# Weight copies tied to a place behind the probabilities' copies, and one transposed key half moved to another bank

## The chip, the cores and the metric

The program runs on one core of a Trainium2 chip. The metric is the device time of one execution in microseconds (us). Three runs of the kernel before gave 1273.09, 1273.96 and 1275.84 us; their median, 1273.96 us, is the time before. PE is the matrix engine, DVE the vector engine, ACT the scalar engine, POOL the general one, SP the queue from which all DMAs here are issued. The work of each engine is done in the order of its own queue; engines wait for each other by semaphores.

## The reference

Two layers work on 256 latent tokens and, in the first layer, 256 context tokens, of width 1024. Each layer is a half-step SwiGLU block, a mixer, and a second half-step SwiGLU block; a modulation from a conditioning vector goes in ahead of each, a residual and a LayerNorm stand behind it. The mixer of the first layer is attention, that of the second a short gated convolution. The change lies in the attention:

```python
qkv = (hx @ w_qkv)                      # 16 heads of 64
q, k = apply_axial_rope(q), apply_axial_rope(k)
qkv_c = (hc @ w_qkv)                    # the context's keys and values
s_win = q k^T * scale + bias, masked    # the neighbourhood: 256 keys with a mask
s_ctx = q k_c^T * scale                 # 256 context keys
p = softmax(concat([s_win, s_ctx]))
o = p[..., :nk] v_blk + p[..., nk:] v_c
y_lat = o.reshape(B, S, D) @ w_out      # the output projection
```

The result is the latent stream, 256 by 1024.

## The kernel before

**Precision.** Every large product is made of two halves: an operand x is split into hi, a copy rounded by the scalar engine, and lo = x - hi, a subtraction on the vector engine. A product is then three matmuls, hi·hi (L159), hi·lo (L160) and lo·hi (L162), added up in one bank of the sums (PSUM). `mmu` issues them: for a pair of row blocks hi·hi and hi·lo twice in turn, then lo·hi twice.

**Weights.** `wunit` (L165) brings one unit of weights: a DMA of 512 KB into a raw tile (tag wr, 4 buffers), two copies of 128x512 on ACT (L181) and two subtractions of 128x512 on DVE (L184). A raw buffer is free for the next DMA when the second subtraction has read it. The DMAs stand in one queue on SP, so one that waits for a raw buffer holds those behind it, the bias tiles' (L738) among them.

**Attention.** The loop at L914 goes over 32 steps, a step being one head and one half of the queries. Scores of two heads (`scores`) go to two banks of the tag "at" (3 banks); the vector engine adds the bias (L830) and takes the maximum (L832), the scalar engine makes the exponentials (L834), the vector engine a reciprocal (L835), and the scalar engine scales the row (L836). Two steps later `probs_T` transposes the probabilities of that step on PE into a bank of the tag "tp" (2 banks) as four 128x128 transposes (L848), and splits them: an ACT copy (L108) and a DVE subtraction (L109). One step on, `values` multiplies them with the values (L860, L861) into a bank of "mm" (3 banks) and adds up two halves (L866, L867).

**What fills PE between.** Between these steps `fill_some` takes matmuls from a generator: first the products for keys and values (`kv_quarter`, names wkv) and queries (`q_half`, wq), then, from step 24 on, the output projection (`last_filler`, wo). A unit of weights is requested where its first matmul is written. `kv_quarter` ends with `rest`, which transposes the keys in two halves j = 0, 1 (kT) into "tp" banks and splits them.

**Order.** The order on PE is the order in which the code is written (manual_schedule). On the other engines a scheduler sets the order: it goes by priorities, and `high_priority` moves weight copies (W_EARLY = 40) and probabilities (P_EARLY = 70) ahead of others. Weight copies so come early or late by what the scheduler believes to be free.

Of the kernel before, what the change touches and what calls it, by code (L numbers as in the profile page):

```python
# [16 lines left out]
P = 128  # L17
# [49 lines left out]
def backbone_kernel(  # L67
# [19 lines left out]
    w_early = [0]  # L87
    ext = [1, 0]
    ada_late = [0]

    def nm(s):
        uid[0] += 1
        return f"{s}_{uid[0]}"

    def act(dt=F32, s="a"):
        return ap.tile([P, 512], dt, tag="act", name=nm(s))

    def bank(tag, s):
        return pp.tile([P, 512], F32, tag=tag, bufs=PB[tag], name=nm(s))

    def mmb(s="mm", t=0):
        return bank("at" if t % 2 else "mm", s)

    def tpb(s="tp"):
        return bank("tp", s)

    def split(src, hi, lo):
        a = nc.scalar.activation(hi, src, AF.Copy)  # L108
        return a, nc.vector.tensor_tensor(out=lo, in0=src, in1=hi.bitcast(F32), op=ALU.subtract)  # L109
# [55 lines left out]
    def wunit(srcs, kn, s):  # L165

        raw = wp.tile([P, UN], F32, tag="wr", bufs=WB[0], name=nm(s + "r"))
        ext[1] += 1
        if ext[0] and ext[1] % (5 + ext[0]) in (E0 if ext[0] == 1 else E2):
            hi = hp.tile([P, UN], F32R, tag="whx", bufs=ext[0], name=nm(s + "h"))  # L170
            lo = hp.tile([P, UN], F32R, tag="wlx", bufs=ext[0], name=nm(s + "l"))
        else:
            hi = wp.tile([P, UN], F32R, tag="wh", bufs=WB[1], name=nm(s + "h"))
            lo = wp.tile([P, UN], F32R, tag="wl", bufs=WB[2], name=nm(s + "l"))
        rv, hv, lv = (t[:, :kn * 512].rearrange("p (a b) -> p a b", a=kn) for t in (raw, hi, lo))
        with tc.high_priority(offset=w_early[0]):
            for src, c in srcs:
                sync.dma_start(rv[:, :, c:c + src.shape[2]], src)
            m = kn * 512
            for a in range(0, m, m // W_HI):  # L180
                nc.scalar.activation(hi[:, a:a + m // W_HI], raw[:, a:a + m // W_HI], AF.Copy)  # L181
            for a in range(0, m, m // W_LO):
                b = a + m // W_LO
                nc.vector.tensor_tensor(out=lo[:, a:b], in0=raw[:, a:b], in1=hi[:, a:b].bitcast(F32), op=ALU.subtract)  # L184
        return hv, lv

    def wrows(w, r0, n, c0, s):
        src = w[r0:r0 + n * P, c0:c0 + 512].rearrange("(k p) n -> p k n", p=P)
        return wunit([(src, 0)], n, s)
# [25 lines left out]
    pt = tpb("ctp")  # L215
# [357 lines left out]
    for q, (k0, n) in enumerate(steps):  # L573
        nxt = start_step(*steps[q + 1]) if q < 4 else iter(())
        for g in range(6):
# [6 lines left out]
            p, j, z = g // 4, g // 2 % 2, g % 2  # L582
# [66 lines left out]
    def sub_end(w, lhs, nk, l, i, gm, wgt, nxt, s, order):  # L649


        gate = mod_rows(l, gm, "gate")
        lnr = None if nxt else ln_rows(l, i)
        GB = fold_cols(nxt[0], 0, nxt[1], (l, i)) if nxt else None
        st, hTs = {}, [None, None]

        def evac(t, n, bank, *c):
            if n == 0:
                st[t] = stat_tile(2 if nxt or t == 0 else 3)
            part = nxt is None and t == n == 1  # L660
            cs = slice(*(c or (0, 512)))
            residual(bank, xt[t][n][:, cs], gate[n][:, cs], wgt, None if c else ALPHA,
                     None if part and not c else st[t][:, n + (c[0] // 256 if c else 0)])
            if n == 1 and (not part or c and c[1] == 512):
                mv, rs = finish_stats(st[t])
                if nxt:
                    hTs[t] = modulated(xt[t], mv, rs, GB, (LN_LAG if nk > KC else LT_LAG)[t], t == 0)
                else:
                    for h in range(2):
                        nc.vector.scalar_tensor_tensor(out=xt[t][h], in0=xt[t][h], scalar=mv[:, 0:1], in1=lnr[0][h],  # L670
                                                       op0=ALU.subtract, op1=ALU.mult)
                    for h in range(2):
                        nc.vector.scalar_tensor_tensor(out=xt[t][h], in0=xt[t][h], scalar=rs, in1=lnr[1][h],
                                                       op0=ALU.mult, op1=ALU.add)
                        sync.dma_start(out[0, t * P:(t + 1) * P, h * 512:(h + 1) * 512], xt[t][h])

        return out_gemm(w, lhs, nk, order, evac, s), hTs, (lambda: new_x(l, i))
# [31 lines left out]
    def rtile(n):  # L709
        if n == 256:  # L710
            return hp.tile([P, n], F32, tag="kr", bufs=8, name=nm("kr"))
        return sp.tile([P, n], F32, tag="s2", bufs=S2, name=nm("qr"))

    def roped(src, t, which, nh):
        n = nh * HD
        C = rope[:, t, 2 * which, :]
        S = rope[:, t, 2 * which + 1, :].rearrange("p (a b e) -> p a b e", a=2, b=2)
        r1 = rtile(n)
        r2 = sp.tile([P, n], F32, tag="tmp", bufs=3, name=nm("r2"))
        nc.vector.tensor_tensor(out=r1.rearrange("p (h d) -> p h d", h=nh), in0=src.rearrange("p (h d) -> p h d", h=nh),  # L720
                                in1=C.unsqueeze(1).to_broadcast([P, nh, HD]), op=ALU.mult)
        bv = src.rearrange("p (h a b e) -> p h a b e", h=nh, a=2, b=2)
        rv = r2.rearrange("p (h a b e) -> p h a b e", h=nh, a=2, b=2)
        for b in range(2):
            nc.vector.tensor_tensor(out=rv[:, :, :, b, :], in0=bv[:, :, :, 1 - b, :],
                                    in1=S[:, :, b, :].unsqueeze(1).to_broadcast([P, nh, 2, 16]), op=ALU.mult)
        nc.vector.tensor_tensor(out=r1, in0=r1, in1=r2, op=ALU.add)
        return r1
# [19 lines left out]
    def tile_panel(c0, c1, hl, s, each):  # L748

        units = []  # L750
        for t, hT in enumerate(hl):
            bk = mmb(s)
            for u in range(KU):
                if t == 0:
                    units.append(wpair(w_qkv, u, c0, c1, s))
                hi, lo = units[u]
                mmu(bk, [(*hsl(hT, UK * u + i), hi[:, i], lo[:, i]) for i in range(UK)], u == 0, u == KU - 1)
                if u == KU - 1:
                    with tc.high_priority(offset=ROPE_EARLY):
                        each(t, bk)  # L760
                yield
                tick()

    def kv_quarter(g, res):
        krs, v = [], []

        def each(t, bk):
            if t < 2:
                krs.append(roped(bk[:, 0:256], t, 1, 4))
            else:  # L770
                r1 = rtile(256)
                nc.scalar.activation(r1, bk[:, 0:256], AF.Copy)
                krs.append(r1)
            v.append(act(F32R, "v"))
            z = v[t].rearrange("p (h s d) -> p h s d", h=4, s=2)
            split(bk[:, 256:512].rearrange("p (h d) -> p h d", h=4), z[:, :, 0], z[:, :, 1])

        yield from tile_panel(D + g * 256, 2 * D + g * 256, [hTs[t] for t in range(4)], "wkv", each)

        def rest():  # L780
            kT = []
            for j in range(2):
                ps = tpb("kT")
                for t in range(4):
                    nc.tensor.transpose(ps[:, t * P:(t + 1) * P], krs[t][:, j * P:(j + 1) * P], ident)
                hi, lo = act(F32R, "kTh"), act(F32R, "kTl")
                split(ps, hi, lo)
                kT.append((hi, lo))
            return kT

        res.append((Late(1, rest), v))
# [50 lines left out]
    def probs_T(h, qt, pr):  # L842
        if h not in PT:
            PT[h] = [hp.tile([P, 4, 256], F32R, tag="pt", bufs=4, name=nm("pT")) for _ in range(2)]
        pth, ptl = PT[h]
        pt = tpb("PT")
        for k in range(4):
            nc.tensor.transpose(pt[:, k * P:(k + 1) * P], pr[:, k * P:(k + 1) * P], ident)  # L848
        split(pt.rearrange("p (k q) -> p k q", k=4), pth[:, :, qt * P:(qt + 1) * P], ptl[:, :, qt * P:(qt + 1) * P])

    osum = {}

# [61 lines left out]
    for i in range(len(steps) + LAG + V_LAG):  # L914
# [24 lines left out]
        j = i - LAG - V_LAG  # L939
# [4 lines left out]
    run(fin)  # L944
    phase.__exit__(None, None, None)
    hTs, later = box
    phase = tc.tile_pool(name="ph2", bufs=1)
    hp = phase.__enter__()
    bias_rows.clear()
# [65 lines left out]
    g, hTs, later = sub_end(sc_w_out[0], lhs_T(yT), KC, 1, 1, 5, 1.0, (1, 6), "wo", order_late(KU))  # L1015
# [57 lines left out]
```

## Time and profile before

| what | us |
|---|---|
| median of three runs | 1273.96 |
| the profiled execution, its own time | 1274.29 |
| span of its trace, first to last instruction | 1272.5 |
| PE idle from 447 to 520 of the span | 0.39 |
| PE idle from 520 to 600 of the span | 8.28 |
| PE idle from 600 to 1272 of the span | 11.20 |

The attention with its fill lies between about 380 and 600 us. The profiled execution stands 0.33 us above the median, and 1.79 us of it lie outside the span. The idle rows are the length of a stretch less PE's busy time in it. A row of a time order gives the start, the duration, the engine, the line, the operation, output<-inputs, and, in brackets, how long the engine was idle just before and what ended that. Matmuls overlap: one of 128x512 shows some 0.39 us, and the next begins some 0.23 us after its start.

### The profile page before, as it was taken

What the parts mean: (1) busy time and instruction counts of PE and PEld (TensorE: products, weight loads), DVE (VectorE), ACT (ScalarE), POOL (GpSimd) and SP (SyncE); (2) the same over time, 40 slices, a digit from 0 to 9 for tenths busy, and PEclk for the clock granted to TensorE, in tenths of its full rate; (3) what the DMA queues carried; (4) which work ended last, traced back from release to release, by engine and by line L of the source; (5) the groups of instructions that cost most, each with busy time, mean ns of one, the idle gap of its engine ahead of it and who ended that gap; (6) DMA issues with size and microseconds to landing.
All of it is one profiled execution on the core that took longest, in us unless ns stands there. A gap on an engine that the chain in (4) does not pass through costs nothing.

```text
span 1272.5 us, 17210 instructions
## 1 busy us (share of the span) xinstructions
PE 1243.8 (98%) x5890; PEld 1005.1 (79%) x5890; DVE 954.3 (75%) x1681; ACT 590.5 (46%) x1148; POOL 42.8 (3%) x71
## 2 busy tenths in 40 slices
PE   7999999999999999988999999999999999999997
PEld 4787778787878777766787788778788887888786
DVE  3699887585868767788997787869776787865545
ACT  2432132412336456686655435645435644655431
POOL 0000000000001111121000000000000000000000
PEclk9999999999999999999999999999999999999999
DMA  9877668484922744464999687779776764776641
GB/s 291 304 232 242 183 211 297 152 289 144 300 90 80 219 91 91 93 150 126 308 319 297 236 292 260 225 222 347 256 259 181 241 205 133 231 226 188 217 160 54
DMA packets 202713, 268.59 MB, mean 211 GB/s; under 512 B 30027, under 2 KB 149299, under 8 KB 202625
## 3 DMA queue, kind: packets, MB, share of 16 engines
q1 hardware_dynamic: 202624, 267.49, 66.7%
q8 instruction: 46, 0.75, 0.2%
q14 instruction: 43, 0.34, 0.1%
HBM read 265.27 MB, written 2.17 MB: 210 GB/s over the span
## 4 chain that ended last, share of the span: by engine, by line
PE 82%; DVE 7%; DMA 6%; ACT 3%; issue 1%; SPq 1%; POOL 0%; DVEq 0%; ACTq 0%; POOLq 0%
PE w L159 15%; PE w L162 15%; PE w L160 15%; PE f L553 6%; PE f L554 6%; PE f L555 6%; DMA w1r<-in_ffn_w_in_dram 3%; DVE w1l L184 2%; PE wkv L159 2%; PE wkv L160 2%; PE wkv L162 2%; PE wc L159 2%; DMA ar<-in_ada_w_dram 2%; PE wc L162 2%; PE wc L160 2%
## 5 line engine op out<-in xcount | busy, mean ns | idle before, releaser
L181 ACT ACTIVATE w1h<-w1r 128x512 fp32r<-128x512 f32 x352 | 202.6, 625 | 174.4 <-PE w L162 70.9
L184 DVE TENSOR_TENSOR w1l<-w1r,w1h 128x512 fp32r<-128x512 f32 x352 | 227.1, 687 | 51.5 <-ACT w1h L181 49.2
L159 PE MATMUL w<-w1h,hTh 128*128 128x512 f32 x528 | 209.8, 397 | 1.4 <-ACT hTh L108 1.4
L252 DVE SCALAR_TENSOR_TENSOR acc<-ar,cst,acc 128x512 f32<-128x512 f32 x266 | 187.1, 749 | 30.2 <-DMA ar<-in_ada_w_dram 30.1
L160 PE MATMUL w<-w1l,hTh 128*128 128x512 f32 x528 | 206.1, 390 | 0.0
L159 PE MATMUL w<-w2h,gh 128*128 128x512 f32 (+1 forms) x446 | 173.4, 389 | 0.0
L160 PE MATMUL w<-w2l,gh 128*128 128x512 f32 (+1 forms) x446 | 172.3, 387 | 0.0
L181 ACT ACTIVATE w2h<-w2r 128x512 fp32r<-128x512 f32 x176 | 101.4, 624 | 137.9 <-PE w L162 129.5
L162 PE MATMUL w<-w1h,hTl 128*128 128x512 f32 x528 | 163.3, 390 | 0.8 <-DVE hTl L109 0.8
L184 DVE TENSOR_TENSOR w2l<-w2r,w2h 128x512 fp32r<-128x512 f32 x176 | 114.1, 688 | 45.7 <-ACT w2h L181 44.8
L553 PE MATMUL f<-h0h,w1h 128*128 128x512 f32 x352 | 139.3, 396 | 0.4 <-ACT w1h L181 0.4
L554 PE MATMUL f<-h0h,w1l 128*128 128x512 f32 x352 | 137.8, 391 | 0.0
L555 PE MATMUL f<-h0l,w1h 128*128 128x512 f32 x352 | 137.7, 391 | 0.0
L162 PE MATMUL w<-w2h,gl 128*128 128x512 f32 (+1 forms) x446 | 136.1, 387 | 0.0
L159 PEld LDWEIGHTS w<-w1h,hTh 128*128 128x128 f32 x528 | 99.2, 188 | 25.4 <-ACT hTh L108 2.7
L162 PEld LDWEIGHTS w<-w1h,hTl 128*128 128x128 f32 x528 | 98.9, 188 | 23.0 <-DVE hTl L109 2.1
L160 PEld LDWEIGHTS w<-w1l,hTh 128*128 128x128 f32 x528 | 99.3, 188 | 19.7 <-DVE w1l L184 0.3
L159 PEld LDWEIGHTS w<-w2h,gh 128*128 128x128 f32 x446 | 83.8, 188 | 18.4 <-ACT w2h L181 0.8
L160 PEld LDWEIGHTS w<-w2l,gh 128*128 128x128 f32 x446 | 83.9, 188 | 16.8 <-DVE w2l L184 0.3
L162 PEld LDWEIGHTS w<-w2h,gl 128*128 128x128 f32 x446 | 83.4, 188 | 17.0
L553 PEld LDWEIGHTS f<-h0h,w1h 128*128 128x128 f32 x352 | 66.4, 189 | 18.6 <-issue 4.6
L555 PEld LDWEIGHTS f<-h0l,w1h 128*128 128x128 f32 x352 | 66.3, 188 | 14.3 <-DVE h0l L531 0.3
(178 smaller groups left out, 1698.8 us busy)
## 6 DMA issues: line engine op xcount, KB each, us to landing
w1r<-in_ffn_w_in_dram SPq DMA_DIRECT2D x352, 256.0 KB
ar<-in_ada_w_dram SPq DMA_DIRECT2D x128, 512.0 KB
w2r<-in_ffn_w_out_dram SPq DMA_DIRECT2D x88, 512.0 KB
ar<-in_ada_w_dram SPq DMA_DIRECT2D x32, 256.0 KB
wkvr<-in_na_w_qkv_dram SPq DMA_DIRECT2D x32, 256.0 KB
wcr<-in_sc_w_in_dram SPq DMA_DIRECT2D x32, 256.0 KB
wqr<-in_na_w_qkv_dram SPq DMA_DIRECT2D x8, 512.0 KB
bias<-in_na_rpb_dram SPq DMA_DIRECT2D x64, 64.0 KB
```

The costliest lines, as they stand in the source:

```text
L159: nc.tensor.matmul(ps, lh, rh, start=first and i == 0, stop=False)
L160: nc.tensor.matmul(ps, lh, rl, start=False, stop=False)
L162: nc.tensor.matmul(ps, ll, rh, start=False, stop=last and i == n - 1)
L181: nc.scalar.activation(hi[:, a:a + m // W_HI], raw[:, a:a + m // W_HI], AF.Copy)
L184: nc.vector.tensor_tensor(out=lo[:, a:b], in0=raw[:, a:b], in1=hi[:, a:b].bitcast(F32), op=ALU.subtract)
L252: nc.vector.scalar_tensor_tensor(out=a, in0=src, scalar=sc, in1=a, op0=ALU.mult, op1=ALU.add)
L553: nc.tensor.matmul(ps, lh, hT0[k][0], start=(k == 0), stop=False)
L554: nc.tensor.matmul(ps, ll, hT0[k][0], start=False, stop=False)
L555: nc.tensor.matmul(ps, lh, hT0[k][1], start=False, stop=(k == KC - 1))
```

## The change

A list `split_behind` holds the two instructions (ACT copy and DVE subtraction) of the latest split of probabilities. `probs_T` writes them into the list each time. `wunit` puts its ACT copies behind the listed ACT copy and its DVE subtractions behind the listed DVE subtraction: an edge that sets the order on that engine alone. The list is empty until the first probabilities are split and is cleared when the attention is over, so every unit that is requested in between is bound: three kinds, wkv, wq and wo. Apart from that the second half of the last quarter's kT gets its bank from "mm" in place of "tp".

```diff
+    split_behind = []
...
-        with tc.high_priority(offset=w_early[0]):
+        with tc.high_priority(offset=w_early[0]), ExitStack() as st:
             for src, c in srcs:
                 sync.dma_start(rv[:, :, c:c + src.shape[2]], src)
             m = kn * 512
+            for i in split_behind:
+                st.enter_context(tc.issue_after(i.ins))
             for a in range(0, m, m // W_HI):
...
-                ps = tpb("kT")
+                ps = mmb("kT") if g == 3 and j else tpb("kT")
...
-        split(pt.rearrange("p (k q) -> p k q", k=4), pth[:, :, qt * P:(qt + 1) * P], ptl[:, :, qt * P:(qt + 1) * P])
+        split_behind[:] = split(pt.rearrange("p (k q) -> p k q", k=4), pth[:, :, qt * P:(qt + 1) * P], ptl[:, :, qt * P:(qt + 1) * P])
...
     hTs, later = box
+    split_behind.clear()
```

The order of the instructions on PE and on POOL is the same in both kernels; on ACT, DVE and SP it is not. In the rows below line numbers of the kernel after are 1 to 3 higher than those of before (L108 is L109, L181 is L184, L184 is L187).

**ACT in the third quarter of keys and values.** On PE the four transposes of PT_711 are followed at once by the products with unit 713 (wkvh_713 from ACT, wkvl_714 from DVE). ACT before, around the copy of PT_711:

```order
L181 ACTIVATE wkvh_713_4131<-wkvr_712_4130 128x512
L772 ACTIVATE kr_693_4054<-wkv_692_4029 128x256
L108 ACTIVATE v_694_4056<-wkv_692_4029 128x4x64
L181 ACTIVATE wkvh_713_4131<-wkvr_712_4130 128x512
L181 ACTIVATE wqh_772_4420<-wqr_771_4419 128x512 x2
L108 ACTIVATE kTh_700_4080<-kT_699_4075 128x512
L108 ACTIVATE kTh_703_4089<-kT_702_4084 128x512
L108 ACTIVATE pT_678_3966<-PT_711_4123 128x4x128
```

and after:

```order
L775 ACTIVATE kr_693_4054<-wkv_692_4029 128x256
L109 ACTIVATE v_694_4056<-wkv_692_4029 128x4x64
L184 ACTIVATE wkvh_709_4109<-wkvr_708_4108 128x512
L109 ACTIVATE kTh_700_4080<-kT_699_4075 128x512
L109 ACTIVATE kTh_703_4089<-kT_702_4084 128x512
L109 ACTIVATE pT_678_3966<-PT_711_4123 128x4x128
L184 ACTIVATE wkvh_713_4131<-wkvr_712_4130 128x512 x2
```

Both copies of unit 713 went from ahead of the copy of PT_711 to just behind it, and unit 772 left the place altogether: it now stands behind the copy of PT_769 and one scaled row of probabilities (pr_762), while PE multiplies with it right behind the transposes of PT_769. Unit 791 stands in the same way behind the copy of PT_789, and 813 behind that of PT_811.

**DVE between the two query panels and the last quarter.** qr_805 is the rotation of the finished panel wq_803 (four instructions); wkvl_810 belongs to the unit with which PE goes on right after that panel. DVE before:

```order
L109 TENSOR_TENSOR pT_768_4410<-PT_804_4564,pT_767_4409 128x4x128
L835 RECIPROCAL mx_799_4537<-mx_799_4537 128x1
L184 TENSOR_TENSOR wkvl_833_4689<-wkvr_831_4687,wkvh_832_4688 128x512
L720 TENSOR_TENSOR qr_805_4583<-wq_803_4551,rope_104 128x512
L725 TENSOR_TENSOR r2_806_4584<-wq_803_4551,rope_104 128x16x16 x2
L184 TENSOR_TENSOR wkvl_833_4689<-wkvr_831_4687,wkvh_832_4688 128x512
L727 TENSOR_TENSOR qr_805_4583<-qr_805_4583,r2_806_4584 128x512
L109 TENSOR_TENSOR pT_788_4493<-PT_811_4605,pT_787_4492 128x4x128
```

and after:

```order
L110 TENSOR_TENSOR pT_768_4410<-PT_804_4564,pT_767_4409 128x4x128
L723 TENSOR_TENSOR qr_805_4583<-wq_803_4551,rope_104 128x512
L728 TENSOR_TENSOR r2_806_4584<-wq_803_4551,rope_104 128x16x16 x2
L187 TENSOR_TENSOR wkvl_810_4592<-wkvr_808_4590,wkvh_809_4591 128x512
L730 TENSOR_TENSOR qr_805_4583<-qr_805_4583,r2_806_4584 128x512
L187 TENSOR_TENSOR wkvl_810_4592<-wkvr_808_4590,wkvh_809_4591 128x512
L110 TENSOR_TENSOR pT_788_4493<-PT_811_4605,pT_787_4492 128x4x128
L187 TENSOR_TENSOR wkvl_814_4614<-wkvr_812_4612,wkvh_813_4613 128x512 x2
```

The subtractions of the first unit of the last quarter, which stood well ahead of this place, now stand behind and within the rotation of the panel that PE has only just finished; those of the second unit stand behind the copy of PT_811.

**ACT in the output projection.** The units are 937, 942, 956, 964, 991, 1000, 1011 and 1016. ACT before, where three of them are copied while the last quarter of keys and values ends:

```order
L181 ACTIVATE woh_942_5177<-wor_941_5176 128x512
L108 ACTIVATE oT_845_4753<-osum_867_4876 128x256
L108 ACTIVATE pT_881_4950<-PT_883_4952 128x4x128
L181 ACTIVATE woh_956_5240<-wor_955_5239 128x512 x2
L181 ACTIVATE woh_964_5277<-wor_963_5276 128x512 x2
L772 ACTIVATE kr_892_4995<-wkv_876_4909 128x256
L108 ACTIVATE v_893_4997<-wkv_876_4909 128x4x64
L108 ACTIVATE pT_877_4916<-PT_894_5000 128x4x128
L108 ACTIVATE pT_881_4950<-PT_895_5007 128x4x128
```

and after, some forty rows further on, where unit 964 is now copied:

```order
L109 ACTIVATE pT_959_5254<-PT_961_5256 128x4x128
L184 ACTIVATE woh_964_5277<-wor_963_5276 128x512
L869 ACTIVATE osum_946_5206<-o_962_5263 64x256
L839 ACTIVATE pr_950_5220<-pr_950_5220,mx_949_5218 128x512
L837 ACTIVATE pr_952_5227,mx_951_5225<-S_948_5210,mx_951_5225 128x512
L109 ACTIVATE oT_910_5076<-osum_946_5206 128x256
L184 ACTIVATE woh_964_5277<-wor_963_5276 128x512
L839 ACTIVATE pr_952_5227<-pr_952_5227,mx_951_5225 128x512
L109 ACTIVATE pT_966_5290<-PT_968_5292 128x4x128
```

The five copies ahead of the copies of PT_894 and PT_895 are gone from there. Each unit now stands behind the probabilities whose transposes PE did last before it: 937 behind PT_914, 942 behind PT_940 (whose transposes are followed at once by its matmuls), 956 behind PT_944, 964 behind PT_961 and with other work between its halves, 991 behind PT_979, 1000 behind PT_995. On SP the DMAs of units 990 to 1015 go to later places, behind bias tiles, since they need the raw buffers of the first four.

## The prediction

> **What bounds the kernel now.** I read the page's engines and chain first, then a table of three stretches, then PE's own waits.
>
> ```profile
> PE 1243.8 (98%) x5890; PEld 1005.1 (79%) x5890; DVE 954.3 (75%) x1681; ACT 590.5 (46%) x1148; POOL 42.8 (3%) x71
> PE 82%; DVE 7%; DMA 6%; ACT 3%; issue 1%; SPq 1%; POOL 0%; DVEq 0%; ACTq 0%; POOLq 0%
> 447.00:520.00 73.00, 72.61 (x385) 58.14 (x384) 56.34 (x120) 47.14 (x104) 10.23 (x12) 1.00 0.48 103
> 520.00:600.00 80.00, 71.72 (x392) 55.35 (x391) 63.03 (x134) 56.57 (x124) 12.55 (x17) 0.98 0.46 108
> 600.00:1272.00 672.00, 660.80 (x3026) 539.80 (x3026) 500.17 (x856) 336.37 (x643) 9.62 (x18) 1.00 0.71 232
> ```
>
> PE sets the end: it is on 82% of the chain. (A stretch's columns are its length, then busy time of PE, PEld, DVE, ACT, POOL, granted clock, DMA share, GB/s.) From 447 to 520, where keys, values and queries fill the attention, PE is idle for 0.39 us only. From 520 to 600, where the output projection does, it is idle for 8.28. So a new wait in the first stretch has no idle time to hide in, and behind 600 PE is idle for 11.2 of 672 us: what the attention loses, the end loses.
>
> The waits at which the change aims are these:
>
> ```profile
> 544.63 0.39 PE L860 MATMUL o<-pT,v 128*128 128x256 f32 x1 [0.75 <-ACT pT L108]
> 545.58 0.39 PE L861 MATMUL o<-pT,v 128*128 128x256 f32 x1 [0.57 <-DVE pT L109]
> 549.95 0.66 PE L785 MATMUL kT<-ident,kr 128*128 128x128 f32 x4 [0.41 <-DVE pT L109]
> 552.16 0.67 PE L785 MATMUL kT<-ident,kr 128*128 128x128 f32 x4 [1.55 <-DVE pT L109]
> 542.43:545.84 3.41, 2.09 (x14) 1.52 (x13) 3.41 (x8) 3.41 (x10) 0.31 (x1) 1.00 0.63 164
> 549.26:552.67 3.41, 1.45 (x11) 0.88 (x9) 3.00 (x7) 3.36 (x9) 0.49 (x2) 1.00 0.85 186
> 552.67:556.08 3.41, 3.41 (x12) 2.27 (x11) 3.41 (x8) 1.88 (x5) 1.19 (x2) 0.50 0.51 65
> 583.41:586.82 3.41, 1.86 (x11) 1.43 (x12) 1.04 (x3) 0.94 (x3) 0.00 (x0) 1.00 0.47 154
> ```
>
> PE waits 0.75 + 0.57 us for copies of probabilities, then 0.41 + 1.55 us for a "tp" bank for kT: 3.28 us. Right behind, the granted clock is 0.50 for 3.41 us, which costs at most half of that, 1.7; I take 1.5. The clock fell behind a stretch of 3.41 us with 1.96 us of idle PE (3.41 - 1.45), and not behind those with 1.32 and 1.55. Five copies of output weights stand ahead of the late probabilities on ACT (541.36 below), so about 4.8 us are there to be won.
>
> **What the change adds: the price of one unit.** The copies of a unit no longer come early; they follow the split of the last transposed probabilities. The rows show that PE uses a unit right behind such transposes:
>
> ```profile
> 530.50 0.60 PE L848 MATMUL PT<-ident,pr 128*128 128x128 f32 x4
> 530.85 0.47 PE L159 MATMUL wkv<-wkvh,hTh 128*128 128x512 f32 x1
> 531.62 0.40 PE L160 MATMUL wkv<-wkvl,hTh 128*128 128x512 f32 x1
> 531.13 0.60 ACT L108 ACTIVATE pT<-PT 128x512 fp32r<-128x512 f32 x1 [0.38 <-PE PT L848]
> 531.76 0.69 DVE L109 TENSOR_TENSOR pT<-PT,pT 128x512 fp32r<-128x512 f32 x1 [2.03 <-ACT pT L108]
> 541.36 2.18 ACT L181 ACTIVATE woh<-wor 128x512 fp32r<-128x512 f32 x4
> 546.11 0.67 DVE L184 TENSOR_TENSOR wol<-wor,woh 128x512 fp32r<-128x512 f32 x1
> 546.77 0.67 DVE L184 TENSOR_TENSOR wol<-wor,woh 128x512 fp32r<-128x512 f32 x1
> ```
>
> Let e be the end of the four transposes (531.10). The first product starts at e - 0.25, the fourth (the second with the low half) at e + 0.52. ACT's copy of the probabilities starts at e + 0.03; four weight copies take 2.18 us, so one follows another every 0.52, and the unit's two end at e + 1.15 and e + 1.67. DVE starts 0.03 behind ACT, at e + 0.66, and gives out one subtraction every 0.6 us (0.66 with a small one between): the unit's end at e + 1.95 and e + 2.55. The fourth product then starts at about e + 2.6 in place of e + 0.52. **One unit used right behind its transposes costs 2.1 us of PE.** About 1.2 + 0.35 us of it show as idle.
>
> **Where that happens.** PE's rows at the five places in the key, value and query panels:
>
> ```profile
> 466.55 0.66 PE L848 MATMUL PT<-ident,pr 128*128 128x128 f32 x4 [0.16 <-DVE kTl L109]
> 466.96 0.47 PE L159 MATMUL wkv<-wkvh,hTh 128*128 128x512 f32 x1
> 492.89 0.60 PE L848 MATMUL PT<-ident,pr 128*128 128x128 f32 x4
> 493.25 0.48 PE L159 MATMUL wq<-wqh,hTh 128*128 128x512 f32 x1
> 499.32 0.60 PE L848 MATMUL PT<-ident,pr 128*128 128x128 f32 x4
> 499.68 0.47 PE L159 MATMUL wq<-wqh,hTh 128*128 128x512 f32 x1
> 508.21 0.39 PE L159 MATMUL wkv<-wkvh,hTh 128*128 128x512 f32 x1
> 509.57 0.60 PE L848 MATMUL PT<-ident,pr 128*128 128x128 f32 x4
> 509.93 0.48 PE L159 MATMUL wkv<-wkvh,hTh 128*128 128x512 f32 x1
> 508.90 0.69 DVE L720 TENSOR_TENSOR qr<-wq,rope 128x512 f32<-128x512 f32 x1
> 509.50 0.75 DVE L725 TENSOR_TENSOR r<-wq,rope 128x256 f32<-128x256 f32 x2
> L836 ACT ACTIVATE pr<-pr,mx 128x512 f32<-128x512 f32 x32 | 22.6, 726 | 0.5 <-DVE mx L835 0.5
> 517.41 0.44 PE L848 MATMUL PT<-ident,pr 128*128 128x128 f32 x2 [0.23 <-DVE qTl L109]
> ```
>
> - Units 713, 791 and 813 (466.96, 499.68, 509.93): 2.1 each, 6.3.
> - Unit 772 (493.25): one scaled row, 726 ns, stands between, and copies of the panel that has just ended keep ACT some 0.3 us longer: 2.1 + 0.6 + 0.3 = 3.0.
> - Unit 809 (508.21): its subtractions stand behind L720 and L725 of the rotation, which cannot start before the panel's end, and one is behind L727 too: 0.6 + 0.7 + 0.6 + 0.6 + 0.7 = 3.2 us from the panel's end to the second low half, where the fourth product would start 0.5 behind it: 2.7.
> - Two old waits go: DVE has fewer weights ahead of kTl and qTl, so 0.16 and 0.23, 0.4.
>
> Sum of the panels: **+11.6**. Nothing covers it: all of it stands in PE's own order.
>
> For the output projection I carry the same durations along ACT's and DVE's new order, with two more:
>
> ```profile
> L834 ACT ACTIVATE pr<-S,mx 128x512 f32<-128x512 f32 x32 | 21.9, 689 | 18.8 <-DVE mx L832 18.7
> L866 ACT ACTIVATE osum<-o 64x256 f32<-64x256 f32 x16 | 6.1, 380 | 6.0 <-PE o L861 5.7
> ```
>
> At the last kT, ACT is freed of four weight copies, but kr and v still wait for the panel's end, so the waits ahead (0.75 + 0.57 + 0.41) shrink by some 0.7 only; the "mm" bank takes the 1.55 away, and the 1.5 of clock go with the idle: 3.8 won. Then the scores, which come at once, wait about 0.9 us for ACT's and DVE's halves of kT, and unit 937 stands behind ACT's kT copy, scaled row, oT, exponential, second kT copy and second scaled row (0.5 + 0.6 + 0.4 + 0.7 + 0.5 + 0.6 = 3.3 us, then its own 0.6 and DVE's 0.7), while PE is there after 2.1: 2.4 late. 3.3 given back, **-0.5**.
>
> From there on each unit is counted from its transposes' end, as above. 942 follows them at once: 2.1, and 0.3 since ACT is still at an exponential, **+2.4**. 964: ACT does pT, the first copy, osum, a scaled row, an exponential, waits for oT (0.5 + 0.5 + 0.4 + 0.6 + 0.7 + 0.5), and only then the second copy (0.6) and DVE its half (0.7); fourth product near e + 4.2, where PE comes at e + 1.4 with eight products of values between: **+2.8**. 1000, with osum and an exponential between its copies: e + 3.4 for e + 1.6, **+1.8**. 991 waits behind a scaled row and osum, but a group of scores lies ahead of it on PE: **+1.6**. 956, with osum between and products and scores ahead: **+0.8**. Units 1011 and 1016 have time, 0. Two old waits go, since PE comes later than the split or the bank it waited for:
>
> ```profile
> 571.49 0.39 PE L861 MATMUL o<-pT,v 128*128 128x256 f32 x1 [0.93 <-DVE pT L109]
> 580.84 0.66 PE L848 MATMUL PT<-ident,pr 128*128 128x128 f32 x4 [0.52 <-DVE pT L109]
> 584.05 0.38 PE L860 MATMUL o<-pT,v 128*128 128x256 f32 x1 [0.92 <-DVE osum L867]
> ```
>
> With PE's restart they are worth 1.2 and 0.6; the third stays, as the one "mm" bank that the projection leaves must be read first. Sum of the projection: -0.5 + 2.4 + 0.8 + 1.6 + 2.8 + 1.8 - 1.8 = **+7.1**. The SP queue costs nothing: units 990 to 1015 are requested only when the subtractions of the first four free their buffers, but each is used over 10 us later.
>
> **The clock.** Unshown is whether the new waits lower it. Three of them (772, 809, 937) hold 2.0 to 2.6 us of idle within about 3 us, as much as the 1.96 that lowered it; a stretch's edge can cut them, so I take two. Bounds: none, 0, and five, at 1.7 each 8.5. I take 2 x 1.4 = **+2.8**, nearest to the row at 552.67.
>
> The Trainium skill, "TensorE: Matmul & The Clock Gate", Part 1, has the clock halve after an idle window of some 3.4 us, and warns of gaps above that. No wait here is that long, so by it no clock falls, and the sum is lower by the 2.8. The trace speaks against its reading as a wholly idle window: a stretch with 1.45 us of busy PE was followed by 0.50.
>
> Sum: 11.6 + 7.1 + 2.8 = 21.5 on the profiled execution's 1274.29 us, which is 0.33 above the median. I forecast 1273.96 + 21.5, rounded to **1295 us**. The bounds of the price of a unit: if only ACT's half is waited for, 1.4 in place of 2.1, eight units save some 6; if DVE's subtractions are slowed as in the group that follows (853 against 688 ns in the clear), eight units cost 2 more.
>
> ```profile
> L184 DVE TENSOR_TENSOR wkvl<-wkvr,wkvh 128x512 fp32r<-128x512 f32 x14 | 11.6, 853 | 1.2 <-ACT wkvh L181 1.2
> ```
>
> **The rivals.**
> - *The units are not needed that soon; the change wins what it aims at.* From 2.6 us between transposes and unit on, a unit costs nothing. Then 3.28 + 1.5 + 0.4 and some of the 1.5 late waits go: 1274 - 6 = 1268. Against it stand the five pairs of rows above, 0.35 us apart. With the case that gains and losses balance, 0.07: 0.04 faster, 0.03 the same.
> - *The clock never falls*, the page's rule: 1274 + 18.7 = 1292.5. For it: stretches with 1.55 us idle kept the clock. 0.2.
> - *The clock falls at most of the long waits*: five times 1.5 = 7.5 for 2.8, 1300. For it: 1.96 us sufficed. 0.15.
> - *The first half alone is waited for, and DVE's is ready*: 1274 + 18.7 - 6 = 1286.5. For it: DVE is free at most of these places; against: its subtraction takes its input from ACT. 0.18.
> - *Only output weights are bound*, as the change's few words have it: 1281. The order rows rule it out: wkv and wq units moved.
>
> **How the numbers follow.** The forecast has 0.40. The range takes the rivals from 1286 to 1300 in, and some 2 us of error at each end: 1284 to 1303. Faster 0.04, the same 0.03, slower 0.93, where 0.2% (2.5 us) is about what a measurement of this kernel can tell.
>
> **What would show it.** Right: PE waits at L159 for ACT (wkvh, wqh, woh) and at L160 for DVE's low halves, above 1 us each, at four places in the panels where it waited nowhere; PE idle from 447 to the end of the panels about 8 us for 0.39; the kT wait of 1.55 gone; a granted clock of 0.50 once to five times. Wrong: no waits on weight copies, or panels as long as before. If the projection's stretch shortens by over 2 us, my count of the waits behind the kT bank is at fault.

## The result and the profile after

| | before | after |
|---|---|---|
| median of six runs each, us | 1273.76 | 1301.42 |
| lowest and highest, us | 1273.09, 1278.37 | 1298.37, 1308.69 |
| ratio to before, 95% interval | | 1.0229, 1.0211 to 1.0247 |
| the profiled execution, its own time, us | 1274.29 | 1300.32 |
| span of its trace, us | 1272.5 | 1298.5 |

The kernel is slower by 27.7 us (by the ratio, 29); the forecast was 21.0 above the median (1295, range 1284 to 1303). The time lies within the range, and the forecast is some 6 us short of it.

The first two lines are from the page of the kernel after (engines, then the chain of waits); the three behind them are stretches of its span in the columns that the prediction named.

```profile
PE 1257.3 (97%) x5890; PEld 1009.7 (78%) x5890; DVE 955.0 (74%) x1681; ACT 592.3 (46%) x1148; POOL 42.2 (3%) x71
PE 86%; DVE 7%; DMA 3%; ACT 2%; issue 1%; POOL 0%; SPq 0%; DVEq 0%; ACTq 0%
447.00:530.00 83.00, 73.44 (x358) 55.94 (x357) 54.23 (x109) 42.88 (x94) 10.31 (x12) 0.96 0.42 94
530.00:564.00 34.00, 33.08 (x190) 26.23 (x189) 22.50 (x55) 21.17 (x49) 5.59 (x7) 1.00 0.32 37
564.00:616.00 52.00, 40.45 (x181) 28.00 (x180) 32.93 (x72) 32.43 (x68) 5.98 (x7) 0.87 0.48 121
```

No engine got more work: DVE and ACT are busy for the same time as before, and PE has as many instructions. Of its 13.5 us more, some 8.5 can be put down to five more stretches at half clock (below; 1.7 each at most), and matmuls right behind a wait show 0.50 us in place of 0.39. What is new stands in the stretches. In the panels (447 to 530) PE is idle for 83.00 - 73.44 = 9.56 us (0.39 before), in the projection (564 to 616) for 11.55, and the granted clock is 0.96 and 0.87 on average.

PE's rows in time order, after, at units 713, 772, 791, 809 and 813, and DVE's and ACT's rows at 713:

```profile
465.38 0.60 PE L851 MATMUL PT<-ident,pr 128*128 128x128 f32 x4
467.19 0.50 PE L160 MATMUL wkv<-wkvh,hTh 128*128 128x512 f32 x1 [1.21 <-ACT wkvh L184]
467.99 0.50 PE L161 MATMUL wkv<-wkvl,hTh 128*128 128x512 f32 x1 [0.30 <-DVE wkvl L187]
469.39 0.28 PE L863 MATMUL o<-pT,v 128*128 128x256 f32 x1
496.83 0.58 PE L160 MATMUL wq<-wqh,hTh 128*128 128x512 f32 x1 [2.34 <-ACT wqh L184]
506.57 0.49 PE L160 MATMUL wq<-wqh,hTh 128*128 128x512 f32 x1 [1.20 <-ACT wqh L184]
518.04 0.50 PE L161 MATMUL wkv<-wkvl,hTh 128*128 128x512 f32 x1 [1.52 <-DVE wkvl L187]
519.77 0.50 PE L161 MATMUL wkv<-wkvl,hTh 128*128 128x512 f32 x1 [1.00 <-DVE wkvl L187]
522.38 0.50 PE L160 MATMUL wkv<-wkvh,hTh 128*128 128x512 f32 x1 [1.21 <-ACT wkvh L184]
466.02 0.60 ACT L109 ACTIVATE pT<-PT 128x512 fp32r<-128x512 f32 x1 [2.53 <-PE PT L851]
466.51 1.14 ACT L184 ACTIVATE wkvh<-wkvr 128x512 fp32r<-128x512 f32 x2
467.25 1.28 DVE L187 TENSOR_TENSOR wkvl<-wkvr,wkvh 128x512 fp32r<-128x512 f32 x2
```

The reader sees the forecast's chain row by row: the transposes end at e = 465.98, ACT's copy of the probabilities starts at e + 0.04, the unit's two copies end at e + 1.67, DVE's subtractions at e + 2.55. From the transposes' start to the values behind the unit it is 469.39 - 465.38 = 4.01 us; in before it was 468.43 - 466.55 = 1.88:

```profile
468.43 0.28 PE L860 MATMUL o<-pT,v 128*128 128x256 f32 x1
```

The difference, 2.13 us, is the price of a unit, where 2.1 was forecast.

The wait of 1.55 us for kT's bank is gone: all eight transposes run as one group without a wait. Behind it the scores wait for the copies of kT, and from there on the units of the projection do:

```profile
563.50 1.09 PE L788 MATMUL kT<-ident,kr 128*128 128x128 f32 x8
565.18 0.50 PE L829 MATMUL S<-kTh,qTh 64*128 64x512 f32 x2 [0.59 <-ACT kTh L109]
566.06 0.51 PE L829 MATMUL S<-kTl,qTh 64*128 64x512 f32 x2 [0.37 <-DVE kTl L110]
568.38 0.51 PE L160 MATMUL wo<-woh,oT 128*128 128x512 f32 x1 [1.59 <-ACT woh L184]
573.65 0.50 PE L160 MATMUL wo<-woh,oT 128*128 128x512 f32 x1 [1.21 <-ACT woh L184]
586.43 0.80 PE L160 MATMUL wo<-woh,oT 128*128 128x512 f32 x1 [1.45 <-ACT woh L184]
```

The clock fell five times. Stretches of 3.41 us of the kernel after (length; then busy time of PE, PEld, DVE, ACT, POOL; granted clock; DMA share; GB/s):

```profile
493.70:497.11 3.41, 1.07 (x7) 0.65 (x5) 1.58 (x4) 3.41 (x9) 0.00 (x0) 1.00 0.50 56
497.11:500.52 3.41, 3.26 (x10) 2.50 (x10) 3.41 (x5) 2.26 (x5) 2.29 (x2) 0.50 0.48 127
503.94:507.35 3.41, 1.92 (x10) 1.15 (x8) 1.39 (x4) 1.64 (x3) 0.00 (x0) 1.00 0.29 98
521.01:524.42 3.41, 1.90 (x8) 1.03 (x7) 2.58 (x5) 3.21 (x7) 0.00 (x0) 1.00 0.40 144
524.42:527.83 3.41, 3.41 (x16) 2.64 (x14) 2.13 (x4) 0.88 (x2) 0.00 (x0) 0.50 0.75 226
585.86:592.69 6.83, 6.26 (x18) 4.06 (x19) 3.17 (x7) 1.73 (x3) 1.76 (x2) 0.50 0.56 159
```

Besides those at 497.11, 524.42 and 585.86 (two stretches in a row) there are falls at 568.79 and 575.62: six stretches of 0.50, where before had one. They stand behind the waits for units 772, 813, 937, 942 and 964.

### The profile page after: what moved, and what is told of

It is laid out like the page before. It is cut to its first block, busy times and chain, and to the rows that moved or that the text cites. A ratio compares the mean times of both kernels' runs of the same rounds, so it can differ in the third digit from the quotient of the medians.

```text
span 1298.5 us, 17201 instructions
## 1 busy us (share of the span) xinstructions
PE 1257.3 (97%) x5890; PEld 1009.7 (78%) x5890; DVE 955.0 (74%) x1681; ACT 592.3 (46%) x1148; POOL 42.2 (3%) x71
## 4 chain that ended last, share of the span: by engine, by line
PE 86%; DVE 7%; DMA 3%; ACT 2%; issue 1%; POOL 0%; SPq 0%; DVEq 0%; ACTq 0%
PE w L160 15%; PE w L163 15%; PE w L161 15%; PE f L556 6%; PE f L557 6%; PE f L558 6%; PE wkv L161 2%; PE wkv L160 2%; PE wkv L163 2%; DVE w1l L187 2%; DMA w1r<-in_ffn_w_in_dram 2%; PE wc L160 2%; PE wc L163 2%; PE wc L161 2%; PE S L829 1%
## 5 line engine op out<-in xcount | busy, mean ns | idle before, releaser
L184 ACT ACTIVATE w1h<-w1r 128x512 fp32r<-128x512 f32 x352 | 202.7, 625 | 170.1 <-PE w L163 62.2
L187 DVE TENSOR_TENSOR w1l<-w1r,w1h 128x512 fp32r<-128x512 f32 x352 | 226.7, 684 | 51.8 <-ACT w1h L184 49.9
L184 ACT ACTIVATE w2h<-w2r 128x512 fp32r<-128x512 f32 x176 | 101.4, 624 | 137.2 <-PE w L163 122.4
L187 DVE TENSOR_TENSOR w2l<-w2r,w2h 128x512 fp32r<-128x512 f32 x176 | 114.0, 686 | 45.7 <-ACT w2h L184 44.8
```

## The experiments

Theories at the start: (A) a unit's price is local, the 2.6 us from transposes to its last low half less what PE has between, and the sum over the units makes the loss; (B) the remainder is the clock, which follows PE's idle time; rivals are that ties crowd ACT and DVE as a whole, that ACT's half alone decides, or that the clock falls for another reason. Each ratio is to the kernel before in the same rounds.

### The bank alone

```diff
-                ps = tpb("kT")
+                ps = mmb("kT") if g == 3 and j else tpb("kT")
```

> The kernel before with only the bank of the second kT half changed; the order on every engine is that of before. Theory: PE's wait of 1.55 us at that half goes, and so does the half clock behind it (about 1.5 us); about 0.9 us comes back where the scores wait for the copies of kT. 1274 - 2.2 = 1271.6, between 1270.5 and 1272.5, and no stretch of clock 0.50 near 553. Rival: the copies of the second half queue behind the same probabilities, so the scores wait as long as the bank did: 1273.8, within 0.7, and the clock falls as before.

Measured: 1272.92 us for 1274.60, ratio 0.9994 (0.9982 to 1.0007): no difference that this can tell. The median lies between the two ranges that I wrote down; by the ratio it is 1273.2 for 1274, in the rival's. PE's rows of this kernel at the place:

```profile
548.60 1.09 PE L785 MATMUL kT<-ident,kr 128*128 128x128 f32 x8 [0.44 <-DVE pT L109]
550.87 0.50 PE L826 MATMUL S<-kTh,qTh 64*128 64x512 f32 x2 [1.18 <-ACT kTh L108]
551.80 0.50 PE L826 MATMUL S<-kTl,qTh 64*128 64x512 f32 x2 [0.42 <-DVE kTl L109]
```

The wait of 1.55 became 1.18 + 0.42 = 1.60 one step later, since the second half's copies stand behind the same probabilities: the rival's mechanism. In the profiled execution the clock did stay at 1.00, as PE's idle time now falls in two stretches (546.82 and 550.24, with PE busy for 2.43 and 2.35 of 3.41 us), but that won too little to be told. So the bank, one of the change's two parts, is worth at most 2.3 us alone (0.0018 x 1274).

### The two kinds of units, each alone

The output projection's units tied, with the bank; then keys', values' and queries' units tied, without it:

```diff
-            for i in split_behind:
+            for i in split_behind if s == "wo" else ():
```

```diff
-            for i in split_behind:
+            for i in split_behind if s != "wo" else ():
...
-                ps = mmb("kT") if g == 3 and j else tpb("kT")
+                ps = tpb("kT")
```

> Only the output projection's units are bound, and the bank is moved; keys', values' and queries' units are free. Theory (the cost of a unit is local to where it is used): the panels run as in before (PE idle from 447 to 520 about 0.4 us), the projection loses what it lost in the changed kernel, 7 us of waits and 3 to 5 of half clock: 1274 + 10 to 13 = 1284 to 1287. Rival (bound units of the panels set ACT and DVE back, and that is what the projection pays): under 1279.

> Only keys', values' and queries' units are bound; the projection's are free, and kT has its old bank. Theory: five units cost 2.1, 3.0 to 3.4, 2.1, 2.7 to 3.4 and 2.1 us, 12 in all, and two stretches of half clock 3.2: 1274 + 15.5 = 1289.5, between 1286 and 1291; together with the run that binds the projection's units alone it makes up the whole loss of the changed kernel (27.7) within 2 us. Rival (the costs overlap): the two sum to under 24 or over 31.

Measured: 1286.40 us, ratio 1.0097 (1.0083 to 1.0111), and 1291.33 us, ratio 1.0130 (1.0116 to 1.0144), both for 1274.60. The second is 1.8 above its 1289.5 and just past the end of what was written, with falls at 498.99, 509.23 and 522.88 (two stretches) besides the one of before: two stretches more than expected. In the first the panels run as before, PE idle for 0.16 us:

```profile
447.00:517.00 70.00, 69.84 (x371) 55.93 (x370) 52.98 (x111) 43.91 (x97) 10.05 (x12) 1.00 0.48 106
```

11.8 + 16.7 = 28.5 us, and the whole change costs 27.7: within what these runs can tell the costs add up, and each lies where its units are used. The rival, overlap, is out. The few words on the change name output weights alone; the other weights carry the greater part.

### Which half sets the price

Only DVE's subtractions tied, ACT's copies free:

```diff
-            for i in split_behind:
+            for i in split_behind[1:]:
```

> The changed kernel with only DVE's subtractions tied behind the probabilities' subtraction; ACT's copies are free to come early again. Theory (the unit's price is set on DVE: its two subtractions end at e + 1.95 and e + 2.55 whether the copies came early or not): units 713, 791 and 813 still cost about 2.1 us each, now as one wait for the low half; 772 some 2.1 and 809 some 3; the time stays at 1294 to 1302. Rival (PE waits for ACT's copies, and DVE is ready when they are): without ACT's part two thirds of the price go, and the time is under 1286.

Measured: 1296.22 us for 1274.29, ratio 1.0174 (1.0158 to 1.0190). PE's and DVE's rows at unit 713 of this kernel:

```profile
465.21 0.62 PE L851 MATMUL PT<-ident,pr 128*128 128x128 f32 x4
465.59 0.47 PE L160 MATMUL wkv<-wkvh,hTh 128*128 128x512 f32 x1
466.50 0.69 DVE L110 TENSOR_TENSOR pT<-PT,pT 128x512 fp32r<-128x512 f32 x1 [0.78 <-ACT pT L109]
467.11 1.28 DVE L187 TENSOR_TENSOR wkvl<-wkvr,wkvh 128x512 fp32r<-128x512 f32 x2
467.84 0.50 PE L161 MATMUL wkv<-wkvl,hTh 128*128 128x512 f32 x1 [1.78 <-DVE wkvl L187]
```

The first product no longer waits, and PE then stands 1.78 us for the low half, which ends at the same distance from the transposes (467.11 + 1.28 = 468.39, e = 465.83: e + 2.56) as with both tied. So DVE's order sets most of the price; what ACT's tie adds is a fifth of the loss (21.9 of 27.7 us remain by the medians; a quarter by the ratios). Unit 809, for which I had expected some 3 us here too, is part of that: its subtractions come ahead of the rotation, and PE does not wait for it. ACT's copies tied alone were not run; since a subtraction takes its input from the copy, I would expect nearly the order of the change itself.

### Distance

Each unit tied to the split before the latest one (the list keeps all of them):

```diff
-            for i in split_behind:
+            for i in split_behind[-2] if len(split_behind) > 1 else ():
...
-        split_behind[:] = split(
+        split_behind.append(split(
```

> The changed kernel, but each unit is tied to the split before the latest one, one head and some 7 us of PE earlier in the panels; the bank is moved. Theory (a unit costs only what is missing from 2.6 us between transposes and use): the five places in the panels cost under 1 us together and the clock stays at 1.00 there; the projection, where steps are shorter, pays some 1 to 4 us at units 937, 991 and 1000; 1274 to 1279. Rival (any tie costs, since the copies crowd behind the probabilities): over 1285.

Measured: 1279.99 us for 1274.29, ratio 1.0047 (1.0030 to 1.0064), 1.0 above the upper end expected. The panels, of this kernel:

```profile
447.00:518.50 71.50, 69.83 (x367) 55.28 (x366) 55.02 (x112) 44.65 (x99) 9.66 (x12) 1.00 0.47 104
```

PE is idle for 1.67 us there, where the latest split as anchor made 9.56, and the clock stays at 1.00. Nearly as many instructions are tied; the place differs. Ties as such cost little here, and a tie just ahead of use costs the whole latency. What is left is the projection, with falls in two stretches from 554.99 on.

### The clock apart from the waits

The changed kernel with products by a zero tile put on PE into its long waits, 51 in all (5, 9, 5, 6 + 4 and 5 in the panels, 6, 5 and 6 at units 937, 942 and 964); they add zeros to sums or write a bank that the next product starts anew.

```diff
+    def zeros(ps, i, first):
+        for _ in range(zfill[i] if zfill else 0):
+            nc.tensor.matmul(ps[0:112], zt, oT[0][0] if uid[0] > 900 else hTs[0].get()[0][0], start=first, stop=first)
...
+            zeros(ps, 2 * i, first and i == 0)
             nc.tensor.matmul(ps, lh, rh, start=first and i == 0, stop=False)
+            zeros(ps, 2 * i + 1, False)
             nc.tensor.matmul(ps, lh, rl, start=False, stop=False)
```

> The changed kernel with products by a zero tile of 112 columns put on PE into its long waits (5 ahead of units 713, 791, 813 and 942, 9 ahead of 772, 6 and 4 ahead of the low halves of 809, 6 ahead of 937 and ahead of the second copy of 964); they add nothing to the sums, and the waits themselves stay as long. Theory (idle time of 1.5 us and more within 3.41 us lowers the clock): with PE busy there the clock stays at 1.00 at the panels and at most falls once in the projection, and the time drops by 6 to 9 us to 1292 to 1296 though nothing is computed earlier. Rival (the clock falls for another reason, or the products delay what follows): 1299 to 1304, with as many stretches of 0.50 as in the changed kernel.

Measured: 1297.59 us for 1274.60, ratio 1.0185 (1.0170 to 1.0201): 3.8 us below the median of the kernel after, 5.6 by the two ratios ((1.0229 - 1.0185) x 1274), and 1.6 above the upper end expected. The same stretch as above, and the only fall that is left, of this kernel:

```profile
493.70:497.11 3.41, 3.13 (x16) 2.10 (x14) 1.56 (x4) 3.41 (x9) 0.00 (x0) 1.00 0.50 55
591.04:594.45 3.41, 2.18 (x8) 1.16 (x8) 3.41 (x9) 2.21 (x5) 0.00 (x0) 1.00 0.01 2
594.45:597.86 3.41, 3.41 (x15) 2.87 (x13) 2.10 (x7) 2.06 (x5) 0.00 (x0) 0.50 0.48 154
```

With PE busy for 3.13 of the 3.41 us the clock stayed at 1.00, although unit 772 came as late as in the kernel after (496.85 for 496.83). At all five places where the clock fell it now stays up; the one stretch of 0.50 that is left stands behind unit 991, where no products were put in. So it is PE's idle time in these waits that let the clock fall, and the kernel is faster for 51 useless products. The four runs lie within 1.3 us at a mean clock of 0.997; the six of the kernel after spread over 10.3, from 1298.37 us at 0.993 to 1308.69 at 0.986. Those 0.007 of 1300 us are 9.1 us of full clock; a stretch at half clock loses 1.7 of it, so by this estimate the runs differ by some five stretches. The median of after is then itself a matter of how many of its waits fall badly; only one of its six runs has a trace.

At a product of the next block, behind the attention (636.92 in after, 631.65 here), the filled kernel is 5.3 us ahead, for five stretches fewer: some 1.1 us each, less than 1.7. At its end it is 3.3 ahead. The other 2 go to waits for the activation (gT waiting for sil), which stands on DVE behind modulation sums that wait for their weights' DMA. PE's waits for sil behind the attention (us in all, times, the longest), before:

```profile
PE gT L412 <- DVE sil L404: 1.9, 3, 1.2
```

The same in the kernel after:

```profile
PE gT L415 <- DVE sil L407: 0.2, 1, 0.2
```

And in the filled kernel:

```profile
PE gT L427 <- DVE sil L419: 2.2, 4, 0.7
```

DVE's row at the longest of them in before, with the DMA that holds it:

```profile
684.76 1.41 DVE L252 SCALAR_TENSOR_TENSOR acc<-ar,cst,acc 128x512 f32<-128x512 f32 x2 [1.39 <-DMA ar<-in_ada_w_dram]
```

So up to some 2 us of what two kernels differ by can go or come here. How late a kernel leaves the attention does not foretell it: over the twelve profiles this wait lies between 0.2 and 2.4 us in no order with that time. The kernel with the bank alone is there 2.5 us earlier than before and waits 1.1 us for 1.9; the filled kernel is there 22 us later than before and waits 2.2.

### Three attempts at a version that beats both

All three have the bank moved. One puts the first unit of the projection between kT's transposes and the scores; one ties units 942, 956 and 964 behind the split of PT_895, well ahead of their use; one does both.

```diff
+        if i == 24:
+            run(fill)
+            KV[3][0].get()
+            fin = last_filler()
+            fill = islice(fin, 9)
+            fill_some(1)
         if i < len(steps) and i % 2 == 0:
```

```diff
+            for i in splits[19] if uid[0] - 1 in (942, 956, 964) else ():
+                st.enter_context(tc.issue_after(i.ins))
```

> The kernel before with the bank moved and, on PE, the first unit of the output projection put between the last kT transposes and the scores that read them; no unit is tied. Theory (the bank alone only moved the wait of 1.55 us to the scores, 1.18 + 0.42): the six products, 1.4 us, cover the copies of kT, so that wait goes for good; 2 to 4 us faster than the kernel before in the same rounds, 1270 to 1272.5. Rival (the wait comes back at the next place, where the probabilities are now late or a unit is missing): within 1 us of before.

> The kernel before with the bank moved and only units 942, 956 and 964 tied, and those behind the split of the last probabilities ahead of kT (PT_895), not behind the latest one. Theory (five copies of these units stood ahead of the late probabilities on ACT): the waits of 0.75, 0.57 and 0.41 us ahead of kT shrink by 0.7 to 1.0 as in the changed kernel, and the units, used 4 to 13 us behind that split, are copied in time; 1 to 3 us faster than before, 1271.5 to 1273.5. Rival (ACT and DVE have no room there, and the copies delay kT's or the scores' work): 1274 to 1278, with new waits at the scores or at unit 942.

> The first unit between the last kT transposes and the scores, the bank moved, and the three next units (with the same products as 942, 956, 964) tied behind the split of the last probabilities ahead of kT. Theory (the waits ahead of kT shrink as with the three units tied, and the unit between takes the place of the wait at the scores): 1 to 2 us below the run with the unit between alone, 1270.5 to 1272, and no wait above 1 us between 540 and 560. Rival (the attention's fill is a fixed stock of nine units, and what is covered early is missing late): within 1 us of the run with the unit between alone, with the waits behind 570 longer by what was won ahead.

> The kernel with the first unit between the last kT transposes and the scores, timed once more to narrow its interval. Theory (the wait at the scores shrank from 1.60 to 0.88 us, a wait of 1.60 came at 580.69, and no stretch of 0.50 is left): 1 to 2 us faster than before, ratio 0.9985 to 0.9995. Rival: no difference, 0.9995 to 1.0005.

| kernel | us | before, same rounds | ratio, 95% interval |
|---|---|---|---|
| unit between | 1272.63 | 1274.29 | 0.9991, 0.9980 to 1.0001 |
| unit between, timed again | 1272.70 | 1273.76 | 0.9993, 0.9981 to 1.0006 |
| three tied | 1274.31 | 1274.29 | 1.0001, 0.9991 to 1.0012 |
| both | 1280.49 | 1273.76 | 1.0046, 1.0030 to 1.0062 |

PE's rows of the kernel with the unit between: the first is the wait that it leaves at the scores, the second the one that it makes 27 us later (0.52 at those transposes in before):

```profile
553.76 0.49 PE L826 MATMUL S<-kTh,qTh 64*128 64x512 f32 x2 [0.46 <-ACT kTh L108]
580.69 0.66 PE L848 MATMUL PT<-ident,pr 128*128 128x128 f32 x4 [1.60 <-DVE pT L109]
```

PE's row at the scores in the kernel with both:

```profile
554.08 0.51 PE L829 MATMUL S<-kTh,qTh 64*128 64x512 f32 x2 [2.70 <-ACT kTh L109]
```

And at the scores in the kernel with three units tied:

```profile
553.59 0.49 PE L829 MATMUL S<-kTh,qTh 64*128 64x512 f32 x2 [1.83 <-ACT kTh L109]
```

The attention has a fixed stock of units to fill with; one spent early is missing late, as the rival had it. If the unit between is faster, it is by some 1 us where 2 to 4 were expected, and both intervals still hold no difference; its first profile shows no stretch of half clock in the attention, its second shows one, at 578.64. The three ties help where they were meant to (0.36 and 0.34 for 0.75 and 0.57 us at the values), but kT's first copy on ACT then stands behind two exponentials, where the bank alone had one ahead of it, and the scores wait 1.83 us for 1.18. With both, two copies of weights stand ahead of kT's first copy as well, the scores wait 2.70 us, and five stretches of half clock follow. For the three ties the rival's range (1274 to 1278) held; for both together neither did. In these two kernels what a tie won at one place was paid at the next that had no room either. No version here is shown to beat the kernel before.

## Why the prediction was right in direction and short in size

- **What bounds, and the price of a unit: right.** 2.1 us forecast, 2.13 measured at 713. The other units read best in the filled kernel, whose clock stays at 1.00 there: from PE's starts there and in before, the delay grows by 2.1 at 713, 3.3 at 772, 2.2 at 791, 3.2 at 809 and 2.2 at 813, and 0.4 goes at qT: 12.6 for 11.6. The term that was off most is 809 (3.2 for 2.7).
- **The kT bank: right that it is given back.** The net of -0.5 up to unit 937 measured -0.3, of which the clock of before is a part.
- **The projection: mechanism right, 2.6 us short.** Measured the same way, 942 costs 3.1 (2.4 forecast), 956 0.8 (0.8), 964 3.4 (2.8), 991 1.8 (1.6); 1000 costs 2.3 in the kernel after, at full clock there (1.8), and 3.2 in the filled kernel, whose own stretch of half clock so makes 0.9. For 964 the durations that I listed add up to e + 4.5, not the e + 4.2 that I used; that alone would have given 3.1. The old waits went as forecast (1.1 and 0.7 for 1.8 together), and a new one of 0.4 at the values came.
- **The clock: the step that failed.** "A stretch's edge can cut them, so I take two": five falls came, six stretches. Of the three units that I named the clock did fall at two, 772 and 937, and an edge did cut the waits at 809. What was wrong is that all other waits were put at nothing: the falls at 813, 942 and 964 make four of the six stretches. I took the 1.96 us of idle time that lowered the clock in before as the bound, and counted only the waits that hold so much. In after, the stretch at 521.01 has 3.41 - 1.90 = 1.51 us of it, a wait of 1.21 and one of 0.30, and that was enough; the stretch at 503.94, with PE busy for 1.92, kept the clock. The rival that I gave 0.15 (1300) is what happened to the clock. Its price at the place is 5.3 us (after against the filled kernel) and the 0.9 of the filled kernel's own stretch, 6.2 together, where 2.8 stood in the sum.
- **"What the attention loses, the end loses": not quite.** 1.7 us come back in the end, most of it between 637 and 738 (PE 27.7 us behind before at the first, 26.1 at the second), as the waits for sil shrink from 1.9 to 0.2 us in these two profiles. That was luck, as the filled kernel's 2.2 us show.
- **The rivals.** That units are not needed so soon is out by the rows above, that only ACT's half is waited for by the run with DVE's tie alone (1296, not under 1286), that only output weights count by the run without them (+16.7). That the clock never falls is out by the five falls. The rule of the Trainium skill, "TensorE: Matmul & The Clock Gate", Part 1, that the clock halves after an idle window of some 3.4 us, read as a window without any work, does not describe these runs: no wait of PE in the attention of the kernel after is longer than 2.34 us, and the clock fell; the measurement decides.

The forecast's 21.5 thus becomes: panels 1.0 more, projection 2.6 more, clock 3.4 more (6.2 for 2.8), 1.7 back behind: 26.8. The two profiled executions differ by 26.0, since PE in the kernel after is already 0.9 us ahead of before at 445, ahead of the first unit that costs; the medians differ by 27.7. All three terms of the cost were too small, and without the 1.7 and the 0.9, which the forecast did not have, the time would have been some 2.6 us longer, 1304, just past the range. That it lies within is in part luck.

## What to carry to other kernels

A tie "behind X" is only as cheap as the time between X and the tied work's first use; count that distance in the trace for every instruction that the rule catches, not just for the few at which it aims, and anchor on an X that lies a step earlier (5.7 us lost here in place of 27.7). On an engine that bounds, waits of 1 to 2 us close together can cost more than their sum, since here they lowered the clock for what followed, and the run times spread. A bank or a slot that removes one wait is worth little until the next reader down the line is shown to be ready.

## What the runs showed of the hardware

I expected one threshold for the clock. Over the twelve profiles of this case, in the stretches of 3.41 us between 440 and 620 us that ran at 1.00, with the edges that the granted clock shows carried along: PE busy for under 1.5 us was followed by 0.50 in 11 of 11; 1.5 to 1.95 us in 10 of 19; 1.95 to 2.45 in 2 of 29; above that in none of 535, in 404 of which PE was busy throughout. Between 1.5 and 1.95, the stretches that were followed by 0.50 saw 5 to 8 matmuls begin (one 10), the others 10 to 13 (two 8): it may be the amount of work and not the busy time that counts, which no run here settles.
